# Retention output product with seven products on half of its rows, the residual stream kept off chip during the mixer

## The chip, the cores and the metric

The kernel runs on one core of a Trainium2 chip. The metric is the device time of one execution in microseconds (us). Three executions of the kernel before took 1260.34 to 1261.17 us, median 1260.89 us. The engines are TensorE (PE; PEld is its weight load), VectorE (DVE), ScalarE (ACT), GpSimd (POOL) and SyncE (SP, which issues most DMAs).

## What is computed

Two decoder layers over 256 tokens of width 1024, in float32. Each layer normalises the residual stream `h`, runs a retention mixer and a state-space mixer side by side, merges them by gates, adds the result to `h`, and then does a gated feed-forward block:

```python
def hybrid_mixer(h, w_in, ret_out, ..., ssd_out, w_o):
    u = h @ w_in
    q, k, v, g_ret, z, xbc, dt, gate_ret, gate_ssd = jnp.split(u, ...)
    ...
    o_ret = yr @ ret_out
    ...
    o_ssd = ys @ ssd_out
    merged = jax.nn.sigmoid(gate_ret) * o_ret + jax.nn.sigmoid(gate_ssd) * o_ssd
    return merged @ w_o

def reference(x, ...):
    h = x
    for l in range(DEPTH):
        h = h + hybrid_mixer(rmsnorm(h, norm_mix_w[l]), ...)
        h = h + swiglu(rmsnorm(h, norm_ffn_w[l]), w_gate_up[l], w_down[l])
    return rmsnorm(h, final_norm_w)
```

The change concerns `o_ret = yr @ ret_out`: 256 tokens x 2048 times 2048 x 1024.

## The kernel before

**Exact products from three.** Every float32 operand is split into a high part (rounded to float32r, on ACT) and the rest (on DVE), and a product is the sum of three matmuls, high-high, high-low and low-high (`mm3`, L538). A matmul has a 128x128 stationary tile of the activations and 512 columns of a weight. Weights are read from HBM in pieces of 128x1024 (512 KB) into `raw` tiles and split on the way: `wh` by ACT (L502), `wl` by DVE (L523). Six split pieces are held at once (`hlS`), and four raw ones (`rawS`).

**Seven products for eight.** Some of the products already use Strassen's scheme in Winograd's form on a 2x2 block partition: the 256 tokens as two halves, eight row tiles of the weight as two quarters of four, 1024 columns as two halves. Seven block products named 11, t1, t2, 22, t3, 21, t4 take the place of eight, and sums of weight quarters and of operand blocks are made beforehand: `sevens` (L355) lays out the pieces, `wino_sums` (L402) makes the weight sums (t1 and t2 by DVE; those listed in `added` by a DMA of the POOL queue that adds into the tile, L412), `seven_sums` (L671) makes the operand sums on DVE and ACT, `seven` (L840) issues the products. `out_wino` (L1031) is the form for a product with sixteen (or more) row tiles, of which eight go by seven products and the others are plain: the state-space output product (`SMID`, L296) and the down projection (`AMID`, L294) use it. A `*` in these lists is one plain row tile, between the products.

**The retention output product** uses `out_job` (L986, called at L1676): 16 row tiles x 2 token halves x 2 column halves x 3 = 192 matmuls of 512 columns. `ret_post` (L1668) multiplies each result by the gate `sgr`. It comes after the four `g` jobs, which make its operand `yr`, and before the four `z` jobs; the state-space products, `ssd` and `wo`, follow.

**Order of the work.** The order is worked out when the program is built: `Flow` (L72) plays each step as a generator with a modelled cost and a priority, and each engine takes the ready step of the lowest priority number. The result is one fixed in-order list per engine; on the chip the engines only wait for each other's semaphores. Jobs are listed in `MIXER` (L1124). Chunk work of the state-space scan (`ssd_chunk`, L1575) has the low priority `lp = pr + 8` (L1564), so it fills what is left. The feeder (L474) issues weight loads on the SP queue in one fixed order, each when its slot is free.

**Memory.** PSUM has six `acc` banks (`accS`) and two `tr` banks (`trS`, for transposes). `h` (L272) stays on chip all the time, two tiles of 128x1024; the decay tables of the retention lie in `cst` (L273) all the time. Operand sums for the mixer's seven products use slots named "C". `ssd_post` (L1743) ends the merge: multiply, add, and transpose (`transposed`, L627) into the operand of `wo`; `add_to` (L1789) adds to `h` and starts the norm of the next block (`Norm.half`, L727).

Of the kernel before, what the change touches and what calls it, by code (L numbers as in the profile page):

```python
# [9 lines left out]
F32 = mybir.dt.float32  # L10
# [6 lines left out]
P = 128  # L17
# [175 lines left out]
def trunk_kernel(  # L193
# [3 lines left out]
    ssd_out, w_o, norm_ffn_w, w_gate_up, w_gf, w_sw, w_dw, w_down, final_norm_w, consts, out,  # L197
# [4 lines left out]
    SLOW = 1500.0  # L202
    ZS_PR = 1.0
    PR0, SLACK = 1.6, 2500.0
    BESIDE = (8, 10, 12, 14, 11, 11, 9, 24, 44)
# [66 lines left out]
    h = [cp.tile([P, D], F32, tag=f"h{t}", name=f"h{t}") for t in range(NT)]  # L272
    cst = cp.tile([P, K_N], F32, tag="cst", name="cst")  # L273
# [22 lines left out]
    SMID = ("*", "*", "11", "*", "t1", "*", "t2", "22", "*", "t3", "21", "t4")  # L296

# [57 lines left out]
    def sevens(w1, w2, added=("t3",), order=ALONE, slots=None):  # L355
# [4 lines left out]
        def add(of):  # L360
# [8 lines left out]
            for q, need, sl in (("11", ("11",), (segS, new_raw_seg)), ("12", ("t1", "t3"), (zS, new_z)),  # L369
                                ("22", ("t2", "22"), (rawS, new_raw)), ("21", ("21",), (rawS, new_raw))):  # L370
                need = [c for c in need if c not in added or c not in ("t1", "t2")]
                for i in range(2):
                    land = holder(held[q, i])
                    if (q, i) == ("11", 1):
                        land = then(land, [wino_sums(i, of, evs, turn, held, part, added, zS) for i in range(2)])
# [26 lines left out]
    def wino_sums(i, job, evs, turn, held, part, added, zS):  # L402
# [51 lines left out]
        fl.release(segS)  # L454
# [254 lines left out]
    class Norm:  # L709


        def __init__(self, w, tag=None):
            self.tag = tag
            self.plain = [[Event() if tag else None for _ in range(NT)] for _ in range(2)]
# [12 lines left out]
        def half(self, t, n, pr):  # L727

            nsl = slice(n * 512, (n + 1) * 512)
            fl.spawn(self.square(t, n, pr))  # L730
            wb = yield self.wb[n]
# [8 lines left out]
            fl.release(silS)  # L740

# [395 lines left out]
    def add_layer_jobs(l):  # L1137
# [15 lines left out]
        for m in MIXERS[l]:  # L1153
            if m == ("ssd",):
# [42 lines left out]
    early_par = Event()  # L1197

    def layer(l, mix, nxt, opening=None):
# [81 lines left out]
        def steps():  # L1281
# [5 lines left out]
            ax, sr, pol, dtt, la = small("ax"), small("sr"), small("pol"), small("dtt"), small("la")  # L1287
# [15 lines left out]
            yield stt(n, pr, dtt, dps, 0.0, pol, ALU.max, ALU.add)  # L1303
            yield stt(n, pr, v3(la), v3(dtt), -1.0, ea.unsqueeze(1).broadcast_to([P, NT, NH]), ALU.mult, ALU.mult)
# [407 lines left out]
        def z_job(g):  # L1712
# [3 lines left out]
            if g == 2:  # L1716
                fl.spawn(seven_sums(zops, yz, (0, 1), "A", at_job[0] + ZS_PR))
# [375 lines left out]
```

## Time and profile before

| | |
|---|---|
| median of three runs | 1260.89 us |
| the profiled execution's own time | 1260.23 us |
| its span in the profile | 1258.2 us |
| granted TensorE clock, mean | 0.999 of full |
| instructions | 17517 |
| moved by DMA | 258.13 MB, 205 GB/s on average |
| POOL busy | 64.4 us |

The span is what the trace covers, from the first to the last instruction; the execution's own time has 2.0 us more around it. Matmuls overlap in the trace (one lasts 0.39 us, the next starts 0.23 us after it), so a PE that is busy all the time can still have gaps between starts: for PE the distance from start to start is read, not the busy time alone.

### The profile page before, as it was taken

The page shows a single profiled execution, that of the slowest core. Times are in us where ns is not written, and L with a number is a line of the kernel's source. Part 1 is how long each engine was busy: PE and PEld are TensorE (multiplying, and loading weights), DVE is VectorE, ACT ScalarE, POOL GpSimd, SP SyncE. Part 2 cuts the span into 40 slices and gives each one's busy share as a digit, 9 for nine tenths or more (in the row PEclk, how much of TensorE's full clock was granted, in tenths as well). Part 3 has the DMA queues.
Part 4 walks back from the last instruction along what each step waited for, and adds up shares of the span by engine and source line. Part 5 has one row for each costly group of instructions (what it writes and reads, how often), then busy time and mean ns, then how long its engine had stood idle before and what let it go on. Part 6 is the DMA issues. An engine that isn't in the chain of part 4 may idle for free.

```text
span 1258.2 us, 17517 instructions
## 1 busy us (share of the span) xinstructions
PE 1247.1 (99%) x6306; PEld 1055.3 (84%) x6306; DVE 1062.3 (84%) x1452; ACT 851.0 (68%) x1271; POOL 64.4 (5%) x84
## 2 busy tenths in 40 slices
PE   9999999999999999999999999999999999999997
PEld 7889888888888788888888898888888887888886
DVE  6998978878589978999788888878875998888996
ACT  6876786987376566776586676967954664766754
POOL 0000000000012001011000000000000110010010
PEclk9999999999999999999999999999999999999999
DMA  8668555555475757886766485555555765678873
GB/s 292 222 176 292 178 175 160 175 189 196 154 281 148 230 177 225 296 225 207 229 210 226 123 266 166 172 192 167 187 199 170 242 189 201 206 226 254 271 202 113
DMA packets 73606, 258.13 MB, mean 205 GB/s; under 512 B 8464, under 2 KB 8720, under 8 KB 73520
## 3 DMA queue, kind: packets, MB, share of 16 engines
q1 hardware_dynamic: 66832, 233.32, 54.6%
q0 software_dynamic: 6400, 23.18, 9.8%
q8 instruction: 49, 0.80, 0.2%
q10 hardware_dynamic: 288, 0.52, 0.1%
q14 instruction: 37, 0.30, 0.1%
HBM read 255.88 MB, written 1.11 MB: 204 GB/s over the span
## 4 chain that ended last, share of the span: by engine, by line
PE 86%; DVE 8%; DMA 3%; issue 2%; ACT 1%; SPq 0%; POOL 0%; POOLq 0%; ACTq 0%; DVEq 0%
PE acc L540 17%; PE acc L539 17%; PE acc L541 17%; PE acc L962 16%; PE acc L963 9%; DVE wl L523 4%; PE tr L636 2%; PE acc L965 2%; PE yps L1623 2%; DVE raws L229 1%; DMA raws<-in_w_sw_dram 1%; DMA raw<-in_w_dw_dram 1%; DMA raw<-in_ssd_out_dram 1%; DVE D L229 1%; DVE plain L229 1%
## 5 line engine op out<-in xcount | busy, mean ns | idle before, releaser
L523 DVE TENSOR_TENSOR wl<-raw,wh 128x1024 fp32r<-128x1024 f32 (+2 forms) x392 | 464.5, 1194 | 76.1 <-ACT wh L502 73.7
L502 ACT ACTIVATE wh<-raw 128x1024 fp32r<-128x1024 f32 (+2 forms) x392 | 400.9, 1036 | 186.2 <-PE acc L541 87.3
L962 PE MATMUL acc<-xT,wh 128*128 128x512 f32 x840 | 304.1, 400 | 0.0
L963 PE MATMUL acc<-xT,wl 128*128 128x256 f32 x960 | 252.2, 281 | 0.0
L539 PE MATMUL acc<-wh,xT 128*128 128x512 f32 (+1 forms) x568 | 219.5, 386 | 0.0
L541 PE MATMUL acc<-wh,xT 128*128 128x512 f32 (+1 forms) x568 | 216.0, 380 | 0.0
L540 PE MATMUL acc<-wl,xT 128*128 128x512 f32 (+1 forms) x568 | 216.0, 380 | 0.0
L963 PEld LDWEIGHTS acc<-xT,wl 128*128 128x128 f32 x960 | 181.2, 189 | 10.1
L962 PEld LDWEIGHTS acc<-xT,wh 128*128 128x128 f32 x840 | 158.0, 188 | 32.3
L540 PEld LDWEIGHTS acc<-wl,xT 128*128 128x128 f32 x568 | 106.7, 188 | 20.1 <-issue 1.0
L539 PEld LDWEIGHTS acc<-wh,xT 128*128 128x128 f32 x568 | 106.7, 188 | 19.5 <-issue 1.2
L541 PEld LDWEIGHTS acc<-wh,xT 128*128 128x128 f32 x568 | 106.7, 188 | 19.5
L502 ACT ACTIVATE wh<-raws 128x1024 fp32r<-128x1024 f32 x80 | 84.1, 1057 | 45.1 <-DVE raws L229 23.6
L523 DVE TENSOR_TENSOR wl<-raws,wh 128x1024 fp32r<-128x1024 f32 x80 | 96.3, 1218 | 9.2 <-ACT wh L502 9.1
L539 PE MATMUL acc<-wh,A 128*128 128x512 f32 x224 | 89.0, 397 | 0.0
L541 PE MATMUL acc<-wh,A 128*128 128x512 f32 x224 | 87.3, 390 | 0.0
L540 PE MATMUL acc<-wl,A 128*128 128x512 f32 x224 | 87.2, 389 | 0.0
L232 DVE SCALAR_TENSOR_TENSOR cc<-cc,cv 128x255 f32<-128x255 f32 (+1 forms) x144 | 68.3, 477 | 11.5 <-ACT cc L222 10.4
L539 PE MATMUL acc<-wh,C 128*128 128x512 f32 (+1 forms) x184 | 72.2, 392 | 0.0
L540 PE MATMUL acc<-wl,C 128*128 128x512 f32 (+1 forms) x184 | 71.2, 387 | 0.5 <-DVE wl L523 0.3
L541 PE MATMUL acc<-wh,C 128*128 128x512 f32 (+1 forms) x184 | 70.7, 384 | 0.0
L541 PEld LDWEIGHTS acc<-wh,A 128*128 128x128 f32 x224 | 42.1, 188 | 9.0
(183 smaller groups left out, 1889.0 us busy)
## 6 DMA issues: line engine op xcount, KB each, us to landing
raw<-in_w_tm_dram SPq DMA_DIRECT2D x104, 512.0 KB, 4.2
raw<-in_w_fm_dram SPq DMA_DIRECT2D x80, 512.0 KB, 4.0
raw<-in_w_gf_dram SPq DMA_DIRECT2D x40, 512.0 KB, 4.7
raw<-in_ret_out_dram SPq DMA_DIRECT2D x32, 512.0 KB, 3.8
raw<-in_w_gate_up_dram SPq DMA_DIRECT2D x32, 512.0 KB, 6.0
raw<-in_w_down_dram SPq DMA_DIRECT2D x28, 512.0 KB, 4.4
raw<-in_w_gr_dram SPq DMA_DIRECT2D x24, 352.0 KB, 3.8
seg<-acs SPq DMA_DIRECT2D x16, 512.0 KB, 5.1
```

The lines of the kernel that those rows point to most:

```text
L229: return dve(n, pr, lambda: nc.vector.tensor_tensor(out=out, in0=in0, in1=in1, op=op))
L232: return Op("dve", 1.04 * n + 130, lambda: nc.vector.scalar_tensor_tensor(out=out, in0=in0, scalar=scalar, in1=in1, op0=op0, op1=op1), pr)
L502: nc.scalar.activation(out=wh[:, :m], in_=raw[:, :m], func=AF.Copy)
L523: nc.vector.tensor_tensor(out=wl[:, :m], in0=raw[:, :m], in1=wh[:, :m].bitcast(F32), op=ALU.subtract)
L539: nc.tensor.matmul(ps, lhsT=lh, rhs=rh, start=first, stop=False, **kw)
L540: nc.tensor.matmul(ps, lhsT=lh, rhs=rl, start=False, stop=False, **kw)
L541: nc.tensor.matmul(ps, lhsT=ll, rhs=rh, start=False, stop=last, **kw)
L636: nc.tensor.transpose(out=ps[:, j * P : (j + 1) * P], in_=src[:, j * P : (j + 1) * P], identity=ident)
L962: nc.tensor.matmul(a, lhsT=wh[:, k % 4, fsl], rhs=x[:, k % 4, :, :], start=k == 0, stop=False)
L963: nc.tensor.matmul(a[:, :SEQ], lhsT=wl[:, k % 4, fsl], rhs=xh[:, k % 4, :], start=False, stop=False)
L965: nc.tensor.matmul(a, lhsT=wh[:, k % 4, fsl], rhs=x[:, k % 4, :, :], start=False, stop=True)
L1623: nc.tensor.matmul(ps[:, i * HD : (i + 1) * HD], lhsT=sg[:, i, :], rhs=xdt[:, i * HD : (i + 1) * HD], start=True, stop=True)
```

## The change

The retention output product goes through `out_wino`: row tiles 0 to 7 by seven products, 8 to 15 plain, in the order `RMID`; 11's raw quarters get two slots of their own (`dec`), which hold the decay tables earlier in the layer. Its operand sums use four new slots "O". `h` lies in two of the "O" slots and gives them up once the norm before the mixer has read it: layer 0 reads it again from `x`, layer 1 writes it to HBM first and reads it back, both on the SP queue, at the start of the `ssd` job. The norm's own operand sums move from "C" to "O". The decay tables are loaded per layer. `ret_post` adds the gated sums that `add_r` left in `gated`. Chunk products of groups 2 and 3 use `tr` banks. The transposes of `ssd_post` are put 800 ns later in the modelled order (`MT_SLACK`). [...]

```diff
-    BESIDE = (8, 10, 12, 14, 11, 11, 9, 24, 44)
+    SLOW, MT_SLACK = 1500.0, 800.0
+    ZS_PR, SAVE, DEC_AT = 1.0, 2000.0, 9000.0
+    BESIDE = (8, 10, 12, 14, 11, 11, 9, 24, 44, 46)
+    decS, new_dec = pooled(tp, (P, D), F32, "dec", 2)
-    bigS = {k: Sem(4) for k in ("A", "C", "D", "Y")}
+    bigS = {k: Sem(4) for k in ("A", "C", "D", "O", "Y")}
-    h = [cp.tile([P, D], F32, tag=f"h{t}", name=f"h{t}") for t in range(NT)]
-    cst = cp.tile([P, K_N], F32, tag="cst", name="cst")
+    h = [None] * NT
+    cst = cp.tile([P, K_DEC], F32, tag="cst", name="cst")
+    RMID = ('*', '*', '*', '*', '11', '*', 't1', '*', 't2', '22', '*', 't3', '21', 't4')
+    RET_FIRST, RET_APART, RET_PR = (decS, new_dec), (), 0.0
...
     class Norm:
+            self.kept = drp.tile([NT, P, D], F32, tag="kept", name="kept", bufs=1) if saved else None
+            self.reads = 8 if saved else 4
...
+        def read(self):
+            self.reads -= 1
+            if not self.reads and self.tag == "O":
+                for t in range(NT):
+                    fl.release(bigS["O"])
+
+        def save(self, t, nsl, pr):
+            yield SAVE
+            yield Op("sp", 450, lambda: nc.sync.dma_start(out=self.kept[t][:, nsl], in_=h[t][:, nsl]), pr)
+            yield fl.transfer(4 * P * 512, 2048)
+            self.read()
...
+            if m == ("ret",):
+                group(sevens(w_rw[l, 0], w_rw[l, 1], added=("t3", "t4"), order=RMID, first=RET_FIRST),
+                      plain((out_srcs(ret_out[l])[8:], RET_APART)))
...
+        def load_decays():
+            if l:
+                yield DEC_AT
+            yield decS
...
-                yield accS
+                yield (trS if g >= 2 else accS)
...
+        def g_job(hd):
+            if hd == 2:
+                fl.spawn(seven_sums(rops, yr, (0, 1), "O", at_job[0] + RET_PR))
+            return tm_job(xT, g_post(hd))
...
         def ret_post(t, n, ps, j):
+            nsl = slice(n * 512, (n + 1) * 512)
+            yield tt(512, j, sgr[t][:, nsl], ps, sgr[t][:, nsl], ALU.mult)
+            fl.release(accS)
+            yield tt(512, j, sgr[t][:, nsl], sgr[t][:, nsl], gated[t].value[:, nsl], ALU.add)
...
+        def add_r(t, n, u, j):
...
+            yield tt(512, j, to[:, nsl], u, sgr[t][:, nsl], ALU.mult)
-        run["ret"] = lambda: out_job(yr, 16, ret_post)
+        run["ret"] = lambda: out_wino(yr, 16, 0, "O", RMID, ret_post, add_r, rops)
...
-            yield from transposed(sgr[t][:, nsl], 4, mT, n, t, j - 1)
+            yield from transposed(sgr[t][:, nsl], 4, mT, n, t, j - 1, slack=MT_SLACK)
...
+        def restore(t):
+            pr = at_job[0]
+            yield bigS["O"]
+            def emit():
+                h[t] = new_big("O", F32, (P, D))
+                nc.sync.dma_start(out=h[t], in_=mix.kept[t] if mix.saved else x[0, t * P : (t + 1) * P, :])
+            yield Op("sp", 450, emit, pr)
...
         def ssd_job():
+            for t in range(NT):
+                fl.spawn(restore(t))
...
             def post(t, n, ps, j):
+                yield h_ev[t]
                 yield tt(512, j - 1, h[t][:, nsl], h[t][:, nsl], ps, ALU.add)
...
-        norms = [Norm(norm_mix_w[0], "C"), Norm(norm_mix_w[1], "C"), Final(final_norm_w)]
+        norms = [Norm(norm_mix_w[0], "O"), Norm(norm_mix_w[1], "O", saved=True), Final(final_norm_w)]
...
+    out["w_rw"] = cols(a["ret_out"][:, :1024], [0, 512], 512, 2)
...
-    nc = _bacc.Bacc("TRN2", target_bir_lowering=False, num_devices=1)
+    nc = _bacc.Bacc("TRN2", target_bir_lowering=False, num_devices=1, dynamic_dma_scratch_size=8192)
```

## Rows read from the trace of the kernel before

**Rows 1.** The page's part 1: busy time, share of the span, instructions.

```profile
PE 1247.1 (99%) x6306; PEld 1055.3 (84%) x6306; DVE 1062.3 (84%) x1452; ACT 851.0 (68%) x1271; POOL 64.4 (5%) x84
```

**Rows 2.** Timeline of PE, layer 0, end of the retention output product; x16 is chunk work.

```profile
320.55 1.89 PE L1623 MATMUL yps<-xdt,seg 128*128 128x64 f32 x16
...
323.03 0.40 PE L539 MATMUL acc<-wh,A 128*128 128x512 f32 x1
...
338.02 0.39 PE L539 MATMUL acc<-wh,xT 128*128 128x512 f32 x1
```

**Rows 3.** Groups of DVE and of ACT by form: busy us, mean ns, idle before.

```profile
L523 DVE TENSOR_TENSOR wl<-raw,wh 128x1024 fp32r<-128x1024 f32 x364 | 441.2, 1220 | 71.3 <-ACT wh L502 68.9
...
L229 DVE TENSOR_TENSOR plain<-plain 128x512 f32<-128x512 f32 x32 | 21.9, 684 | 2.0 <-ACT plain L222 2.0
...
L229 DVE TENSOR_TENSOR raws<-raws,cc 128x1024 f32<-128x1024 f32 x16 | 19.5, 1216 | 0.0
...
L502 ACT ACTIVATE wh<-raw 128x1024 fp32r<-128x1024 f32 x364 | 380.6, 1057 | 175.9 <-PE acc L541 82.8 <-DMA raw<-in_w_tm_dram 16.3 <-PE acc L962 13.3
...
L222 ACT ACTIVATE sx<-acc 128x512 f32<-128x512 f32 x30 | 17.7, 590 | 4.8 <-PE acc L541 4.7
```

**Rows 4.** Busy time by stretch: PE, PEld, DVE, ACT, POOL, clock, DMA share, GB/s.

```profile
260.00:280.00 20.00, 20.00 (x115) 17.38 (x115) 13.92 (x23) 16.27 (x35) 0.00 (x0) 1.00 0.46 155
280.00:325.00 45.00, 45.00 (x234) 37.74 (x233) 35.55 (x43) 28.89 (x44) 0.00 (x0) 1.00 0.61 200
325.00:345.00 20.00, 20.00 (x90) 16.57 (x89) 10.26 (x11) 6.70 (x7) 0.00 (x0) 1.00 0.40 127
345.00:380.00 35.00, 35.00 (x164) 29.09 (x164) 29.97 (x42) 24.58 (x37) 4.90 (x7) 1.00 0.77 276
380.00:424.00 44.00, 43.40 (x200) 35.75 (x198) 42.91 (x52) 28.66 (x37) 6.71 (x7) 1.00 0.65 180
...
901.00:946.00 45.00, 45.00 (x235) 37.72 (x234) 35.21 (x43) 27.82 (x43) 0.00 (x0) 1.00 0.59 194
946.00:966.00 20.00, 20.00 (x90) 16.56 (x89) 10.09 (x11) 7.03 (x7) 0.00 (x0) 1.00 0.39 135
```

**Rows 5.** Timeline of PE at the merge of either layer, brackets: idle before.

```profile
423.01 0.39 PE L541 MATMUL acc<-wh,C 128*128 128x512 f32 x1
424.46 0.63 PE L636 MATMUL tr<-cst,D 128*128 128x128 f32 x4 [1.06 <-DVE D L229]
...
1044.65 0.39 PE L541 MATMUL acc<-wh,C 128*128 128x512 f32 x1
1045.96 0.63 PE L636 MATMUL tr<-cst,D 128*128 128x128 f32 x4 [0.92 <-DVE D L229]
```

**Rows 6.** The chain of waits ahead of those transposes: start, us, what.

```profile
396.43 2.27 DVE raws L229 x2
...
408.41 7.54 DMA raw<-in_ssd_out_dram
...
1024.35 9.59 DMA raws<-in_w_sw_dram
```

**Rows 7.** Timeline of PE inside the state-space product's seven products, layer 1.

```profile
1036.19 0.39 PE L541 MATMUL acc<-wh,Y 128*128 128x512 f32 x1
1036.59 0.50 PE L539 MATMUL acc<-wh,Y 128*128 128x512 f32 x1
```

**Rows 8.** DMA issues by line: how many, size, median us to landing.

```profile
cc<-in_w_sw_dram POOLq DMA_DIRECT2D x4, 512.0 KB, 5.5
raws<-in_w_sw_dram POOLq DMA_DIRECT2D x4, 512.0 KB, 8.2
```

**Rows 9.** Timeline of POOL in the state-space output product, layer 0.

```profile
390.27 0.90 POOL L412 DMA_DIRECT2D cc<-in_w_sw_dram  x1
...
400.98 0.86 POOL L412 DMA_DIRECT2D raws<-in_w_sw_dram  x1 [8.88 <-DVE wl L523]
403.00 0.86 POOL L412 DMA_DIRECT2D raws<-in_w_sw_dram  x1 [1.17 <-DVE wl L523]
```

More of the change, by code (lines that the diff above doesn't have):

```diff
@@ L196, in trunk_kernel @@
     x, x_t, norm_mix_w, w_tm, w_gr, w_fm, conv_p, steps_p, ret_out, ssd_norm_w,
[L197 removed]
+    ssd_out, w_o, norm_ffn_w, w_gate_up, w_gf, w_rw, w_sw, w_dw, w_down, final_norm_w, consts, out,
 ):
@@ L353, in add_job, with sevens @@
         group(plain((srcs, apart)))
-    def sevens(w1, w2, added=("t3",), order=ALONE, slots=None):
+    def sevens(w1, w2, added=("t3",), order=ALONE, slots=None, first=None):
         def add(of):
@@ L368, in add @@
             got_specs = []
-            for q, need, sl in (("11", ("11",), (segS, new_raw_seg)), ("12", ("t1", "t3"), (zS, new_z)),
+            for q, need, sl in (("11", ("11",), first or (segS, new_raw_seg)), ("12", ("t1", "t3"), (zS, new_z)),
                                 ("22", ("t2", "22"), (rawS, new_raw)), ("21", ("21",), (rawS, new_raw))):
@@ L374, in add @@
                     if (q, i) == ("11", 1):
-                        land = then(land, [wino_sums(i, of, evs, turn, held, part, added, zS) for i in range(2)])
+                        land = then(land, [wino_sums(i, of, evs, turn, held, part, added, zS, (first or (segS,))[0]) for i in range(2)])
                     got_specs.append((min(at[c, i] for c in need) - (0.01 if q == "12" else 0),
@@ L400, in then, with wino_sums @@
         return run
-    def wino_sums(i, job, evs, turn, held, part, added, zS):
+    def wino_sums(i, job, evs, turn, held, part, added, zS, xS):
         pr = job - 0.7
@@ L1398, in retention @@
             fl.release(accS)
+            heads_left[0] -= 1
+            if not heads_left[0]:
+                fl.release(decS)
             yield act(3 * P, pr, ph, prb, AF.Copy)
@@ L1436, in layer @@
         heads = [(Event(), Event(), Event()) for _ in range(RH)]
+        heads_left, decays = [RH], Event()
+        def load_decays():
[3 more added lines that the diff above has]
+            def emit():
+                d = new_dec()
+                nc.sync.dma_start(out=d, in_=consts[:, K_DEC:])
+                return d
+            d = yield Op("sp", 450, emit, -1)
+            fl.transfer(4 * P * D)
+            fl.set(decays, d)
+        if l:
+            fl.spawn(load_decays())
+        else:
+            first_decays.append(load_decays)
         def q_job(hd):
@@ L1768, in layer, with emit @@
         zops = {q: Event() for q in ALONE}
+        h_ev = [Event() for _ in range(NT)]
+        def restore(t):
+            pr = at_job[0]
+            yield bigS["O"]
+            def emit():
+                h[t] = new_big("O", F32, (P, D))
+                nc.sync.dma_start(out=h[t], in_=mix.kept[t] if mix.saved else x[0, t * P : (t + 1) * P, :])
+            yield Op("sp", 450, emit, pr)
+            yield fl.transfer(4 * P * D)
+            fl.set(h_ev[t])
         def ssd_job():
@@ L1784, in seven_job @@
         def seven_job(kind, c, added):
+            if kind == "z":
+                z_begins(c)
             return wino_job(mix.ops, posts_of[kind](c), posts_of[kind](c + 1))
@@ L1990, in whole @@
         yield from opening.slots()
+        for t in range(NT):
+            yield bigS["O"]
+            h[t] = new_big("O", F32, (P, D))
         def constants(lo, hi):
```

54 lines of the change are left out of this document (34 added, 20 removed).

## The prediction

> **What bounds the kernel now.** The page's first part comes first: PE is busy for 1247.1 of 1258.2 us, DVE for 84%, ACT for 68% [rows 1]. A busy PE may still have gaps, so the second view is PE's timeline. From 323.03 to 338.02 us there are 66 steps from start to start: 0.227 us for a matmul of 512 columns, and nothing between them [rows 2]. PE is the bound, at its own pace: a matmul less is 0.227 us less, as long as whatever feeds PE keeps up. [...]
>
> **The sum, step by step.** *Matmuls.* Before: 16 row tiles x 4 x 3 = 192 per layer. After: 8 x 4 x 3 = 96 plain and 7 products x 4 row tiles x 3 = 84, together 180. Over two layers 24 fall away: 24 x 0.227 = **-5.45 us**, all on the path. [...]
>
> *Work on DVE and ACT, per layer.* DVE: 22 pieces are split instead of 16, 6 x 1.22 = 7.3 us; t1 and t2 of two pieces each, 4 x 1.22 = 4.9; operand sums, 12 steps x 0.68 = 8.2 (four to join the parts, four sums, four low parts); two subtractions, four gatings in add_r and four more additions in ret_post, 10 x 0.68 = 6.8: 27.2 us in all [rows 3]. ACT: 6 x 1.06 + 7 x 0.59 = 10.5 us [rows 3], against 29.4 us idle from 280 to 345 [rows 4]: nothing. For DVE the cover is its idle time from 260 to 380 us, 30.3 us, less the 2.7 us by which the stage shrinks: 27.6 [rows 4]. So 27.2 fit into 27.6, if the chunk work of groups 2 and 3 gives way into the stretches behind; it has the lowest priority and is wanted only by z2 and z3, behind z0 and z1. That is the narrow point of the change. What PE loses by it lies between nothing and the whole of what cannot move (first rival). The nearest row is another stage of the same kind under a fuller DVE: within the seven products of the state-space output, PE's longest step is 0.40 instead of 0.227 us [rows 7]. I take about two such, 0.4 us per layer: **+0.8 us**.
>
> *Merge.* There PE's gaps are 1.45 and 1.31 us from start to start [rows 5], so 2.3 us above its pace are lost. MT_SLACK moves the transposes 0.8 us back in the modelled order, so a step of three matmuls (0.68 us) goes ahead of them, perhaps two. One each: **-1.4 us**, between 0 and -2.3. What is late next is wo, whose operand these transposes make; plain work of the state-space product still stands before it. In return DVE enters 380 us with less slack behind it: the chain into these transposes runs over DVE sums and over DMAs that took 7.54 and 9.59 us [rows 6], and every microsecond of DVE work left over from the retention product ends there. Between 0 and some 2 us per layer; I take 0.5: **+1.0 us**.
>
> *Transfers.* Plain bytes of ret_out stay equal (8 pieces and 8 quarter pieces for 16). New per layer are two loads of h (1.05 MB) at the start of ssd, in layer 1 also four saves of h and one load of the decay tables. At 276 GB/s for a share of 0.77 [rows 4], the two loads of h take 2.9 us of all DMA engines; the stretch from 380 to 424 has 35% of its DMA time free [rows 4]. So 0, with 2.9 us per layer as the other end. On SP they stand in front of the pieces that ssd and wo still want. Their slots have been free since the end of the retention product, so SP does not stand still for them; the saves wait for DVE's last addition to h, behind which layer 1's weights queue, but they are ordered 2 us after it, and six split and four raw pieces cover a hitch there. h is wanted only when wo ends. On POOL's queue come four adding DMAs per layer; POOL is otherwise idle from 260 to 345 us [rows 4]. They land 5.5 and 8.2 us after issue [rows 8]; t3 and t4 stand last in the order and have that time. [...] Issue took 0.86 us both for the first and the second of a pair 2.0 us apart [rows 9], so nothing waits now; the other end is a second one that starts only when the first has landed, 6.2 us later. I take 0, the value of those rows.
>
> *Banks.* Chunk products in the `tr` banks hold one for 1.9 us [rows 2] and a DVE step of 0.68: transposes behind it could lose up to 2.6 us per layer, and the freed `acc` banks are what the seven products need. Nothing either way. The last plain row tile is 12 matmuls, 2.7 us, in which add_r must free a bank for z0: one or two DVE steps, so nothing.
>
> Sum: -5.45 + 0.8 - 1.4 + 1.0 = **-5.05 us**. The profiled execution took 1260.23 us in all (span 1258.2 and 2.0 around it); it becomes 1255.2. The median of the runs lies 0.66 us above that execution, so the forecast is **1255.8 us**.
>
> **Rivals.** *DVE becomes the bound in the retention product (slower).* Operand sums, splits and weight sums, 20.4 us, are due before the last product starts. In 280 to 325 us only 9.5 are idle [rows 4]; the 6.1 us before it are scattered while the operands are still being made. If the chunk work does not give way, for instance because its buffers (four `sx`, also used by the operand sums and by the products' copies) are held in the wrong order, PE waits up to 10.9 us per layer: -5.45 + 21.8, 1277.2 us. At half of it, 5.5 us per layer, -5.45 + 11.0, the time is 1266.4. It decides from 4.0 us of waiting per layer on. For it: the fit of 27.2 into 27.6. Against it: DVE is idle for 9.7 us directly behind the stage in both layers, and the state-space stage runs with 1.1 us idle of 44 and loses next to nothing within its products [rows 4, 7].
>
> *The gain is given back at the merge (no change).* The left-over work, 2 us per layer, runs through z and ssd, where DVE has no room, and the later transposes don't help: -5.45 + 0.8 + 4.0, so 1260.2. For it: the chain there is DVE's from 396 us on [rows 6]. Against it: 5.0 us are idle from 345 to 380 [rows 4].
>
> *The adding DMAs come late (no change).* POOL's issues of 0.86 to 0.90 us were made while DVE was busy for 42.9 of 44 us [rows 4, 9], so they weren't held up visibly. If each of the eight were held by one DVE step of 1.22 us, and a pair's second by the first's, half of 9.8 us would show on PE: -5.05 + 4.9, 1260.7. [...]
>
> *h or the weights come late, or the change takes out less than it counts (no change).* 2.9 us per layer: -5.05 + 5.8, 1261.6. That fewer than 24 matmuls go is hardly possible, as the lists are fixed when the program is built.
>
> **How the numbers follow.** About 0.2%, 2.5 us, can be told from no change. Forecast 0.66 (1253 to 1258.3; its low end takes all of the merge's 2.3 us and no new loss: -7.75, 1253.1); gain given back at the merge 0.16; adding DMAs late 0.03; transfers late or nothing taken out 0.03; DVE the bound 0.12. Faster therefore 0.66, within 0.2% 0.22, slower 0.12. The range from 1253.0 to 1263.0 leaves out the first rival and little of the forecast's own low end. The forecast's own range is 1253.0 to 1258.3.
>
> **What would show it.** Right: PE's instructions fall by 24, from 6306 to 6282; PE's steps in the retention product stay at 0.227 us with single steps up to 0.4; DVE's busy time grows by about 54 us, and from 260 to 424 us it is idle for 2 or 3 us; the gap before the merge's first transposes falls below 1 us. Wrong: waits of PE for `wl` pieces or for operand sums in the retention product (first rival), a gap of more than 3 us at the merge (second), ACT or DVE waiting for the adding DMA's tile ahead of t3 or t4 (third), SP standing at the saves or loads of h.

## The result, and the profile after

The changed kernel takes 1263.13 us (median of 22 runs, 1260.83 to 1265.72); the kernel before 1260.20 us (22 runs). The ratio is 1.0021, 95% interval 1.0015 to 1.0027: **slower by 0.2%**, where 5 us less were forecast. The profiled execution took 1262.38 us, its span is 1260.5 us (before: 1258.2). What follows is read from that execution; it lies 0.75 us below the median of the 22.

First the page's part 1 of the changed kernel, beside [rows 1]:

```profile
PE 1244.5 (99%) x6282; PEld 1049.6 (83%) x6282; DVE 1106.7 (88%) x1516; ACT 873.7 (69%) x1299; POOL 73.9 (6%) x92
```

The 24 matmuls are gone (6306 to 6282), and DVE has 44.4 us more. So the saving was made, and something took more than it back. Where it went is read from PE's timeline, by two stages in each layer: **stage A** from the first matmul of the retention output product to the first of the state-space product (the retention product and the four z jobs), **stage B** from there to the first matmul of `wo` (the state-space product and the merge). The marks of stage A in layer 0, of the kernel before:

```profile
284.09 0.39 PE L539 MATMUL acc<-wh,Y 128*128 128x512 f32 x1
...
384.26 0.39 PE L539 MATMUL acc<-wh,C 128*128 128x512 f32 x1
```

and of the changed kernel:

```profile
283.81 0.39 PE L544 MATMUL acc<-wh,A 128*128 128x512 f32 x1
...
385.95 0.39 PE L544 MATMUL acc<-wh,C 128*128 128x512 f32 x1
```

Stage A took 384.26 - 284.09 = 100.17 us before and takes 102.14 after, though it has 12 matmuls less, 2.72 us at 0.227. The same marks in layer 1 give 100.22 and 102.81. **So 4.7 and 5.3 us are lost in stage A, 10.0 us together.** Stage B became shorter, 43.89 to 42.58 us and 44.02 to 42.68, 2.65 us together. -5.45 + 10.0 - 2.65 = +1.9 us; the span grew by 2.3, so 0.4 us lie outside the two stages.

What PE waits for stands in its waits (engine, line, released by: us in total, times, longest, over the whole execution); the changed kernel:

```profile
PE acc L544 <- ACT sx L222: 4.5, 2, 2.9
PE acc L545 <- DVE wl L528: 1.5, 4, 0.7
...
PE ips L1662 <- DVE xdt L229: 1.0, 2, 0.9
```

The first is new and the largest: once per layer PE stands until ACT has copied a bank (`sx`), in the middle of the product t4. PE's timeline at the two places (brackets: idle before, and who ended it):

```profile
326.07 0.39 PE L546 MATMUL acc<-wh,Y 128*128 128x512 f32 x1
328.08 0.50 PE L544 MATMUL acc<-wh,Y 128*128 128x512 f32 x1 [1.62 <-ACT sx L222]
...
948.27 0.39 PE L546 MATMUL acc<-wh,Y 128*128 128x512 f32 x1
951.58 0.50 PE L544 MATMUL acc<-wh,Y 128*128 128x512 f32 x1 [2.92 <-ACT sx L222]
```

From start to start these are 2.01 and 3.31 us, 4.9 us above PE's pace: half of the loss. Of the other half, PE's remaining waits in stage A (one for a `wl` in z0, at 340.29, two for the scan's `xdt`, two for an operand from ACT) take 2.4 us, four more transposes per layer 0.6, and some 2 us are single steps longer by hundredths and tenths of a microsecond, with no wait recorded ahead of them. The copy is not slow (0.58 us); it is late. ACT's timeline in layer 0 shows what stands ahead of it in ACT's list:

```profile
304.80 1.06 ACT L507 ACTIVATE wh<-raw 128x1024 fp32r<-128x1024 f32 x1 [1.21 <-DMA raw<-in_w_rw_dram]
...
312.82 1.06 ACT L507 ACTIVATE wh<-raw 128x1024 fp32r<-128x1024 f32 x1 [4.20 <-DMA raw<-in_ret_out_dram]
...
319.76 1.06 ACT L507 ACTIVATE wh<-raw 128x1024 fp32r<-128x1024 f32 x1 [1.16 <-DMA raw<-in_w_rw_dram]
322.21 1.06 ACT L507 ACTIVATE wh<-raw 128x1024 fp32r<-128x1024 f32 x1 [1.39 <-PE acc L545]
323.18 1.99 ACT L507 ACTIVATE wh<-dec 128x1024 fp32r<-128x1024 f32 x2
325.19 1.28 ACT L222 ACT_TABLE_LOAD   x1
326.48 1.06 ACT L222 ACTIVATE seg<-seg 128x1024 f32<-128x1024 f32 x1
327.44 0.58 ACT L222 ACTIVATE sx<-acc 128x512 f32<-128x512 f32 x1
```

Three times ACT stands for a weight piece that has not landed (1.21, 4.20 and 1.16 us; in layer 1 the second of these is 5.71). When it goes on, it has splits, a table load and the scan's exponential to do before the copy, since its list is fixed. The pieces are late because their loads are issued late; SP's timeline:

```profile
285.33 0.33 SPq L489 DMA_DIRECT2D raw<-in_ret_out_dram  x1
294.44 6.07 SPq L489 DMA_DIRECT2D raw<-in_w_rw_dram  x2
308.86 0.33 SPq L489 DMA_DIRECT2D raw<-in_ret_out_dram  x1
...
311.13 4.36 SPq L489 DMA_DIRECT2D raw<-in_w_rw_dram  x2
```

The piece that ACT waits for until 312.82 was asked for at 308.86. The row at 294.44 is two loads; the second, the last before 308.86, went out at 300.18. A load goes out when a raw slot is free, and a slot is free when DVE has made `wl` of the piece in it. DVE's timeline:

```profile
290.93 1.22 DVE L528 TENSOR_TENSOR wl<-dec,wh 128x1024 fp32r<-128x1024 f32 x1
292.06 1.22 DVE L229 TENSOR_TENSOR dec<-dec,raw 128x1024 f32<-128x1024 f32 x1
293.20 1.22 DVE L528 TENSOR_TENSOR wl<-raw,wh 128x1024 fp32r<-128x1024 f32 x1
294.33 1.22 DVE L229 TENSOR_TENSOR dec<-dec,raw 128x1024 f32<-128x1024 f32 x1
...
298.93 1.22 DVE L528 TENSOR_TENSOR wl<-raw,wh 128x1024 fp32r<-128x1024 f32 x1
...
307.61 1.22 DVE L528 TENSOR_TENSOR wl<-raw,wh 128x1024 fp32r<-128x1024 f32 x1
```

Each of the three loads follows the end of such a `wl` at once (293.20, 298.93 and 307.61, each plus 1.22). One round of a slot can be read from these lines: load issued at 300.18, ACT's split begun at 304.80 and done at 305.86, `wl` begun at 307.61 and done at 308.83, next load at 308.86. Of these 8.7 us the load took 4.6, the split 1.1, `wl` itself 1.2, and 1.75 us are DVE's delay, as it had other steps to do first. And there are few slots: the two quarters "12" stay in two of the four raw slots until t1 and t3 have been made from them, so all other retention pieces go through the two that are left. **The reading**: two rotating slots, with a round of 8.7 us of which a DVE that is behind makes 1.75; late loads; ACT's list held up; the copy, and PE, late. Part of the lateness is in the transfers: the load at 311.13, beside an adding DMA that POOL issued at 310.26, was in flight for 8.6 us, until ACT could split it at 319.76, and in the kernel before no load of this product took more than 5.3 us. No run separates that part.

DVE's and ACT's room is in the view by stretch, in the columns of [rows 4]; the changed kernel:

```profile
260.00:280.00 20.00, 20.00 (x115) 17.39 (x115) 16.79 (x24) 16.05 (x33) 0.00 (x0) 1.00 0.64 224
280.00:325.00 45.00, 44.88 (x219) 36.79 (x218) 40.95 (x53) 33.36 (x47) 4.05 (x5) 1.00 0.69 196
325.00:345.00 20.00, 17.73 (x77) 13.82 (x76) 19.62 (x24) 14.22 (x21) 0.00 (x0) 1.00 0.58 190
345.00:380.00 35.00, 34.84 (x176) 28.86 (x175) 33.41 (x48) 23.80 (x37) 5.93 (x7) 1.00 0.83 278
380.00:424.00 44.00, 44.00 (x203) 36.56 (x203) 43.38 (x54) 29.01 (x38) 6.68 (x7) 1.00 0.72 209
```

In the 164 us DVE is busy for 154.2 and idle for 9.9. It was never "full" as a sum; it is full where it counts, 19.62 of 20 us behind t4, and late before. At the merge the waits of [rows 5] are gone: the first transposes follow a matmul after 0.24 us in layer 0, and after 0.30 in layer 1.

```profile
425.41 0.39 PE L546 MATMUL acc<-wh,C 128*128 128x512 f32 x1
425.65 0.63 PE L641 MATMUL tr<-cst,D 128*128 128x128 f32 x4
```

### The profile page after: what moved, and what is told of

It is laid out like the page before. It is cut to its first block, busy times and chain, and to the rows that moved or that the text cites. A ratio compares the mean times of both kernels' runs of the same rounds, so it can differ in the third digit from the quotient of the medians.

```text
span 1260.5 us, 17612 instructions
## 1 busy us (share of the span) xinstructions
PE 1244.5 (99%) x6282; PEld 1049.6 (83%) x6282; DVE 1106.7 (88%) x1516; ACT 873.7 (69%) x1299; POOL 73.9 (6%) x92
## 4 chain that ended last, share of the span: by engine, by line
PE 80%; DVE 8%; ACT 4%; DMA 4%; issue 3%; SPq 0%; POOLq 0%; POOL 0%; ACTq 0%; DVEq 0%
PE acc L545 16%; PE acc L544 16%; PE acc L546 16%; PE acc L986 14%; PE acc L987 8%; DVE wl L528 4%; DMA raw<-in_w_tm_dram 2%; PE tr L641 2%; PE acc L989 2%; PE yps L1675 2%; ACT wh L507 2%; DVE D L229 1%; DVE raws L229 1%; DMA raw<-in_w_dw_dram 1%; PE ips L1662 1%
## 5 line engine op out<-in xcount | busy, mean ns | idle before, releaser
L507 ACT ACTIVATE wh<-raw 128x1024 fp32r<-128x1024 f32 (+2 forms) x388 | 396.8, 1035 | 154.2 <-PE acc L546 27.3
L507 ACT ACTIVATE wh<-raws 128x1024 fp32r<-128x1024 f32 x80 | 84.2, 1057 | 41.1 <-DVE raws L229 22.2
L544 PE MATMUL acc<-wh,C 128*128 128x512 f32 (+1 forms) x152 | 59.3, 390 | 0.2 <-ACT wh L507 0.2
L545 PE MATMUL acc<-wl,C 128*128 128x512 f32 (+1 forms) x152 | 58.4, 384 | 0.3 <-DVE wl L528 0.2
L546 PE MATMUL acc<-wh,C 128*128 128x512 f32 (+1 forms) x152 | 58.2, 383 | 0.0
```

The costliest lines, as they stand in the source:

```text
L507: nc.scalar.activation(out=wh[:, :m], in_=raw[:, :m], func=AF.Copy)
L544: nc.tensor.matmul(ps, lhsT=lh, rhs=rh, start=first, stop=False, **kw)
L545: nc.tensor.matmul(ps, lhsT=lh, rhs=rl, start=False, stop=False, **kw)
L546: nc.tensor.matmul(ps, lhsT=ll, rhs=rh, start=False, stop=last, **kw)
```

## The experiments

Fifteen kernels, each timed beside the kernel before on the same chip (11 runs each, but 4 of e3, 5 of e7, e13 and e15, and 7 of e4 and e8). "Loss in A" is the time of stage A in both layers above 194.92 us, which is twice 100.18 (the plain product) less twice 2.72. All figures are of the profiled executions, but for the ratio. One execution of a kernel differs from another by 1 us and more: the profiled one lies 3.4 us above the median of its kernel's runs in e4, 2.2 in e7, 1.2 in e8, 1.1 in e15 and 0.8 in e11, and 0.8 us below it in e6. So the loss in A of e4 and of e7 is that of a long execution.

| kernel | A, layer 0 and 1 | loss in A | B, layer 0 and 1 | span | ratio to before, interval |
|---|---|---|---|---|---|
| changed | 102.14, 102.81 | 10.0 | 42.58, 42.68 | 1260.5 | 1.0021 [1.0015, 1.0027] |
| e1, plain | 100.17, 100.22 | | 42.79, 42.74 | 1256.7 | 0.9994 [0.9985, 1.0003] |
| e2, plain | 100.18, 100.45 | | 42.88, 42.52 | 1256.4 | 0.9994 [0.9985, 1.0003] |
| e3 | 111.08, 109.91 | 26.1 | 43.62, 43.76 | 1277.3 | 1.0164 [1.0150, 1.0178] |
| e4 | 102.88, 104.15 | 12.1 | 43.52, 42.67 | 1263.3 | 1.0025 [1.0013, 1.0036] |
| e5 | 100.22, 99.96 | 5.3 | 44.85, 43.40 | 1256.9 | 0.9990 [0.9981, 0.9998] |
| e6 | 100.06, 101.11 | 6.3 | 42.56, 42.59 | 1255.8 | 0.9989 [0.9980, 0.9998] |
| e7 | 104.30, 104.66 | 14.0 | 42.51, 42.71 | 1264.1 | 1.0035 [1.0022, 1.0048] |
| e8 | 101.89, 100.30 | 7.3 | 44.69, 45.63 | 1263.2 | 1.0029 [1.0017, 1.0040] |
| e9 | 102.11, 102.58 | 9.8 | 42.57, 42.86 | 1259.4 | 1.0014 [1.0005, 1.0023] |
| e10, plain | 100.18, 100.48 | | 42.52, 42.58 | 1254.9 | 0.9980 [0.9971, 0.9989] |
| e11 | 99.40, 98.46 | 2.9 | 44.67, 43.91 | 1256.1 | 0.9977 [0.9969, 0.9986] |
| e12 | 99.94, 99.28 | 4.3 | 44.15, 44.91 | 1257.1 | 0.9993 [0.9984, 1.0002] |
| e13 | 98.60, 98.03 | 1.7 | 44.82, 42.70 | 1253.0 | 0.9961 [0.9949, 0.9974] |
| e14, plain | 100.18, 100.23 | | 42.54, 42.54 | 1255.0 | 0.9978 [0.9969, 0.9987] |
| e15 | 99.27, 99.69 | 4.0 | 42.57, 42.57 | 1254.3 | 0.9965 [0.9953, 0.9978] |

A limit: e5, e8, e10 and e12 change what the planner sees, so the whole order of the work is another, beside the one size changed. No run has a fifth slot in the changed kernel's own order. In e4 and e7 the order of the product itself is edited. e6, e9 and e15 keep every engine's list of the changed kernel, e11 and e13 that of e5, and e14 that of e10, but for the widths of DVE's steps.

### What the other parts of the change do

**e1: the kernel before with the later transposes alone.**

```diff
-            yield from transposed(sgr[t][:, nsl], 4, mT, n, t, j - 1)
+            yield from transposed(sgr[t][:, nsl], 4, mT, n, t, j - 1, slack=800.0)
```

> The kernel before with the 0.8 us on the merge's transposes alone. The merge's gain is separate from the rest: PE's gaps before the first transposes (1.45 and 1.31 us in the kernel before) fall below 0.5 us and the time falls by 2 to 2.7 us, a ratio near 0.998. Rival: the step only moves the wait to the product behind it (wo), and the time stays within 0.5 us of the kernel before.

Stage B falls by 1.1 and 1.28 us, 2.4 together, and the span by 1.5: the step does about what the changed kernel shows at the merge. The time fell less than expected: the ratio was to be near 0.998, and at 0.9994 it can't be told from no change.

**e2: the changed kernel with the plain retention product.**

```diff
-        run["ret"] = lambda: out_wino(yr, 16, 0, "O", RMID, ret_post, add_r, rops)
+        run["ret"] = lambda: out_job(yr, 16, ret_post)
```

> The changed kernel with the retention output product as 16 plain row tiles again; the residual stream off chip, the tables per layer, the tr banks and the later transposes stay. Theory that the loss is all in the new product and its surroundings: as fast as the kernel before with the later transposes alone, ratio 0.998 (within 0.6 us of it). Rival, the residual stream's transfers or the tr banks cost: 1 to 5 us more than that, ratio 0.999 to 1.002.

Stage A is that of the kernel before (100.18 and 100.45), and the span is e1's within 0.3. So the residual stream off chip, the tables per layer and the chunk products in the `tr` banks cost nothing that shows, and **the loss belongs to the seven products**.

### Attempts on the wait for the copy

**e3: the held quarters "12" in `cc` slots, so that all four raw slots rotate.**

```diff
-                group(sevens(..., order=RMID, first=RET_FIRST),
+                group(sevens(..., order=RMID, first=RET_FIRST, slots=(ccS, new_cc)),
```

> The changed kernel with the retention's held quarters (12) loaded into the two cc slots instead of two of the four raw slots. Theory 'late pieces' (held quarters leave two raw slots, ACT waits for weights, 4.2 and 5.7 us, and reaches the copy that t4 needs too late): those waits of ACT fall below 1.5 us, the gaps before t4 (2.0 and 3.3 us) fall below 0.6, and 4 to 6 us come back: 1257 to 1259 us, ratio 0.9975 to 0.999. Theory 'DVE is full': no change, 1263, ratio 1.002. Theory 'scan work ahead of the copy': the gaps before t4 stay above 1.5 us, ratio 1.001 to 1.002.

Far worse. SP's timeline says why: the `cc` slots are held by the convolutions then, and SP, which issues in a fixed order, stands at that load with all later pieces behind it.

```profile
276.69 26.35 SPq L489 DMA_DIRECT2D cc<-in_w_rw_dram  x2
```

This answers nothing about the slots; it shows what a late piece costs when it stands first in the queue.

**e4: a plain row tile between 21 and t4 instead of ahead of 11**, so that PE has 2.7 us of other work while ACT comes to the copy.

```diff
-    RMID = ('*', '*', '*', '*', '11', '*', 't1', '*', 't2', '22', '*', 't3', '21', 't4')
+    RMID = ('*', '*', '*', '11', '*', 't1', '*', 't2', '22', '*', 't3', '21', '*', 't4')
```

> The changed kernel with one plain row tile moved from the front to between 21 and t4, so that the copy has 2.7 us more. Both 'late pieces' and 'scan work ahead of the copy': the gaps before t4 (2.0 and 3.3 us) go, 3 to 5 us come back (1258 to 1260, ratio 0.9985 to 1.0), while ACT's waits for weights stay. 'DVE is full': the wait only moves, to t4's weights or to z0: 1262 to 1264, ratio 1.0015 to 1.003.

The wait for the copy goes, and PE waits for weights instead:

```profile
PE acc L545 <- DVE wl L528: 4.3, 7, 1.0
```

Five of the seven waits, 3.4 us, stand in stage A, and two of 0.63 us for ACT's split beside them. The wait was the place where lateness came out, not its source. How much the move is worth this trace doesn't tell: its execution took 1265.38 us, the longest of seven (median 1261.99), and has a stretch at a lower granted clock in it, 0.72 (last section).

**e7: the sum for t1 too by an adding DMA, which takes two of DVE's sums per layer away.**

```diff
-                group(sevens(..., added=("t3", "t4"), order=RMID, first=RET_FIRST),
+                group(sevens(..., added=("t1", "t3", "t4"), order=RMID, first=RET_FIRST),
```

> The changed kernel with t1 of the retention product also made by an adding DMA, so that the held quarters (12) are loaded only for t3 and occupy no raw slot before; DVE has 2 additions (2.3 us) less per layer. 'Late pieces': ACT's waits for the plain pieces and the gaps before t4 fall below 1 us, 4 to 6 us come back: 1257 to 1259 us, ratio 0.9975 to 0.999. 'DVE is full': 1 to 2 us come back, ratio 1.0005 to 1.0015. If the longer row of DMAs (load 12, add 22) is late, the gap stands before t1 or t3 instead and the time stays at 1262 or more.

Slower: the weights of t3 and z0 come late then (5.6 us in four waits for `wl`), and ACT waits 8.0 and 8.9 us for quarter pieces. DVE's work was swapped for DMA latency.

**e8: the scan's last group started with z0 instead of with the retention product.**

```diff
-            if jj == 1:
+            if jj == 1 and g < 3:
...
+                fl.spawn(ssd_group(3))
```

> The changed kernel with the scan work of group 3 started with z0 instead of after its xs job, out of the retention product. 'Scan work ahead of the copy': the gaps before t4 fall below 0.6 us; the waits in z (0.2 to 0.9 us before the scan's products) grow by 1 to 3 us; 1260 to 1263 us. 'Late pieces': ACT still waits 4 us and more for the plain pieces; the gaps shrink by the 2.3 us of table load and exponential at most; 1261 to 1264 us. 'DVE is full': about 10 us of DVE work leave the stage, so its waits go and come back in z2 and z3, 1262 to 1268 us.

The waits for the copy fall to 0.63 us in each layer, but the same scan work comes back as waits in z and the state-space product: stage B is 2.1 and 2.95 us longer than in the changed kernel. So the scan's exponential ahead of the copy is not enough of a cause by itself.

### Slots and DVE

**e5: five raw slots**, and with them half the room for the descriptors of POOL's DMAs, 4096 bytes instead of 8192.

```diff
-    HB, RB, TAIL, WARM = 6, 4, 5, 2
+    HB, RB, TAIL, WARM = 6, 5, 5, 2
...
-    nc = _bacc.Bacc("TRN2", target_bir_lowering=False, num_devices=1, dynamic_dma_scratch_size=8192)
+    nc = _bacc.Bacc("TRN2", target_bir_lowering=False, num_devices=1, dynamic_dma_scratch_size=4096)
```

> The changed kernel with five raw slots instead of four (its 4 KB from the descriptor room, 4096 bytes). 'Late pieces' (two of four raw slots hold quarters, so loads wait for splits): SP issues the plain pieces of the retention product earlier, ACT's waits for them (4.2 and 5.7 us) and the gaps before t4 fall below 1 us, 3 to 6 us come back: 1257 to 1260 us, ratio 0.9975 to 1.0. 'DVE is full': 1262 to 1264 us, ratio 1.0015 to 1.003. If the smaller descriptor room costs anything, POOL's issues take more than 0.93 us or adding DMAs land later than 8 us, and everything gets slower.

The wait for the copy is gone, and so are ACT's for the plain retention pieces; the loss in A falls from 10.0 to 5.3 us, by the slot together with the order that goes with it. What PE waits for now is DVE's scan operands in stage A, and weights in stage B:

```profile
PE ips L1662 <- DVE xdt L229: 2.7, 3, 1.4
PE acc L545 <- DVE wl L528: 1.4, 2, 0.8
```

**e9: the smaller descriptor room alone** (the last line of that diff).

> The changed kernel with the descriptor room of POOL's DMAs at 4096 bytes instead of 8192, and nothing else: every engine's list is the same. The run with a fifth raw slot had this smaller room too. If its gain of 4.5 us against the changed kernel is the slot's (with the new order that goes with it), this kernel stays with the changed one: span 1260.5 us within 1, the two waits of PE for ACT's copy ahead of t4 still there (1.6 and 2.9 us in the changed kernel). If the smaller room had a part in it, the waits are shorter and the span is below 1259 us.

The two waits for the copy stay (1.42 and 2.31 us), and so does the loss in A, 9.8 us; the span, 1259.4, lies 0.1 us outside the expected band. The room has no part in e5's gain.

**e10: five slots with the plain product** (e2 and e5 together), the control.

> Control: a fifth raw slot and the smaller descriptor room, with the retention product left as plain (16 row tiles), beside the residual stream off chip, the tables and the later transposes. If the slot mends what the seven products brought into the retention product, it gives nothing here, where nothing waits: span 1256.4 us within 0.8, as in the run with the plain product and four slots. If the slot helps any kernel of this kind, the span falls by 2 us or more, and the gain of the run with the fifth slot says nothing of the new product.

Neither answer whole: the span falls by 1.5 us, but stage A doesn't move (100.18 and 100.48). The gain is at the start of the program: the retention product of layer 0 begins at 282.56 us instead of 283.89 (282.19 to 283.28 in the six kernels with five slots, 283.38 to 284.64 in the others). So of e5's 3.6 us of span some 1.5 are that, and within stage A the slot helps the seven products alone, by 4.7 us. This is also the fastest kernel here that computes all of the reference.

**e6: lighter sums on DVE, four slots.** DVE's sums for t1 and t2 and its four operand sums are made on 8 columns, by the author's estimate 7 us of DVE less per layer.

```diff
-                yield tt(D, pr, x, x, w, ALU.add)
+                yield dve(D, pr, lambda n=8 if xS is decS else D: nc.vector.tensor_tensor(out=x[:, :n], in0=x[:, :n], in1=w[:, :n], op=ALU.add))
...
-            yield tt(512, pr, out, a, b, op_)
+            yield dve(512, pr, lambda ..., n=512 if tag != "O" or plain else 8: ...)
```

> The changed kernel with every engine's order kept and DVE's work shortened: the additions for t1 and t2 and the four operand sums of the retention product touch 8 columns instead of 1024 and 512, 4 x 1.15 + 4 x 0.6 = 7 us of DVE less per layer (those sums are left out of the result). 'DVE is full': the gaps before t4 (2.0 and 3.3 us) and in z go, 4 to 8 us come back: 1255 to 1259 us, ratio 0.9955 to 0.999. 'Late pieces' by slots and transfers alone: less than 1.5 us comes back, 1261.5 to 1263, ratio above 1.0005. Both together (loads wait for slots that DVE frees late): 2 to 5 us.

The copy's wait goes in layer 0 and halves in layer 1, and the loss in A falls to 6.3 us, though ACT still stands for the two retention pieces:

```profile
ACT wh L507 <- DMA raw<-in_ret_out_dram: 11.3, 2, 5.8
```

So in layer 0 the late piece alone no longer makes PE wait for the copy; in layer 1 it still does, for 1.4 us. With every list kept, this is what DVE's load alone is worth: 3.8 us. It does free the slot earlier, the load of the late piece in layer 0 goes out at 305.87 instead of 308.86; but that load is in flight longer, and ACT starts on it at 311.74 instead of 312.82.

**e11: both cures** (e5 and e6 together).

> Both cures together: the fifth raw slot, and DVE's sums for t1 and t2 and its four operand sums of the retention product on 8 columns instead of 1024 or 512 (that part of the product's sums is left out of the result; DVE's list is that of the run with the fifth slot). If the whole loss is the supply of weights and operands by a full DVE, the two cures take away the waits that are left (PE for DVE's xdt and wl, 4 us in the run with the fifth slot), and the span is 1252 to 1254 us. If one cure only does what the other does, 1255.5 to 1257 us. If something else than the supply holds PE (the retention products themselves at a longer step), also 1255.5 or more, with no waits of PE above 0.5 us left from 280 to 385 us.

The cures add for the most part: the loss in A is 2.9 us (5.3 and 6.3 with one of them), so 7.1 us come back, where 4.7 and 3.8 would make 8.5. But the span is 1256.1 us, in the band of "one does what the other does": stage B became 44.67 and 43.91, where the backlog now comes out. By the span of this one execution the run would have been misread; the ratio, 0.9977 against 0.9990 and 0.9989, shows some of the second cure.

**e12: five slots and the scan's last group later** (e5 and e8 together), an attempt at a better version.

> A version that may beat both: the fifth raw slot, and the chunk work of the scan's last group started with z0 instead of with the retention product. With five slots the longest wait left in layer 0 is PE's for DVE's xdt of the chunk work, 1.39 us inside the retention product. If the chunk work is in the way there, that wait goes and the span falls from 1256.9 to about 1255 us. If the same DVE work only comes later, as it did with four slots, the waits stand in the z and state-space products instead: 1256.5 to 1259 us.

As e5: less loss in A, the waits in stage B instead.

**e13 and e14: much room on DVE, with seven products and with the plain product.** To e11 and to e10 is added that the scan's and z's steps that work in place take 8 columns.

```diff
-            yield tt(1024, lp, sg, sg, cb[:, 2 * t, :].unsqueeze(1).broadcast_to([P, HPG, P]), ALU.mult)
+            yield tt8(1024, lp, sg[:, 0, :], sg[:, 0, :], cb[:, 2 * t, :], ALU.mult)
...
-                yield tt(512, j, sil, sil, y, ALU.mult)
+                yield tt8(512, j, sil, sil, y, ALU.mult)
```

> Five raw slots and a DVE with room: as the run with both cures, and besides in each layer the scan's steps that work in place (its 1024-wide multiplication, and of the 512-wide ones four per group) and z's two multiplications per result on 8 columns, some 30 us of DVE less per layer; every other engine's list is the same, and those parts of the scan, of z and of the retention sums are left out of the result. P is the span of its pair, the plain product with the same room on DVE. If the loss is the supply by a full DVE, wherever it shows, the 24 matmuls now bring what they are worth: P - 4.5 to P - 5.5 us (24 x 0.227 = 5.45). If the seven products cost PE something else (longer steps by themselves, ACT's list, weights from HBM, the start of the product), the span is P - 2 or more, as it was P + 1.2 with both cures.

> The pair of the run before: the plain retention product with five raw slots, and the same steps of the scan and of z on 8 columns (left out of the result); every other engine's list as in the control with the plain product. PE waited for next to nothing in that control, so room on DVE should give nothing by either theory: span 1254.9 us within 0.8. If the span falls by 2 us or more, DVE costs the plain product's kernel something too, and the pair is to be read by its difference alone.

The view by stretch over stage A, first of e13, then of e14:

```profile
284.00:333.00 49.00, 48.88 (x229) 40.13 (x229) 43.11 (x60) 39.13 (x52) 4.05 (x5) 1.00 0.73 215
333.00:385.00 52.00, 52.00 (x266) 43.74 (x265) 36.14 (x67) 35.08 (x58) 4.59 (x8) 1.00 0.55 201
```

```profile
284.00:333.00 49.00, 49.00 (x252) 41.05 (x251) 25.24 (x39) 24.61 (x38) 0.00 (x0) 1.00 0.53 172
333.00:385.00 52.00, 52.00 (x243) 43.24 (x242) 37.83 (x58) 34.98 (x51) 6.11 (x8) 1.00 0.74 253
```

The plain product gains nothing from the room (1255.0, as expected). With seven products stage A is 1.58 and 2.20 us shorter than its pair's, 3.8 of 5.45 us, and the loss there is 1.7. The span is 2.0 us below its pair's, where the second answer begins: by it the 24 matmuls don't yet bring what they are worth. The difference is in stage B of layer 0, 2.3 us longer than the pair's: there PE waits twice for a `wl`,

```profile
398.39 0.39 PE L544 MATMUL acc<-wh,A 128*128 128x512 f32 x1
399.42 0.50 PE L545 MATMUL acc<-wl,A 128*128 128x512 f32 x1 [0.64 <-DVE wl L528]
```

as it does in e5 and e11, whose order this is. It is not in stage B of e15, with another order and the same room, so it goes with the planner's order for five slots; why there was not tried.

**e15: the same room with four slots, in the changed kernel's own order** (e6 with the edits of e13).

> The changed kernel with its own four raw slots, with DVE's room of the two runs before and the light sums; every other engine's list is that of the changed kernel. If slots are scarce only because DVE frees them late, this kernel does about as well as the one with five: within 1.5 us of it, and ACT's waits for the late retention pieces (5.5 and 5.8 us with the light sums alone) and PE's for the copy ahead of t4 are gone. If two rotating slots are too few by themselves, ACT still waits over 3 us for those pieces and the span stays at 1254 us or more.

Mixed. The span is within 1.3 us of e13's, and the medians, 1254.93 and 1254.76 us, don't differ by more than the runs of one kernel do. PE's wait for the copy is gone in layer 0 and is 1.37 us in layer 1. ACT still stands for the retention piece in both, 4.70 and 5.44 us. The profile puts the first down to PE, but the piece itself landed at 311.82, 0.1 us before ACT went on. ACT's timeline:

```profile
311.93 1.06 ACT L507 ACTIVATE wh<-raw 128x1024 fp32r<-128x1024 f32 x1 [4.70 <-PE acc L545]
...
930.72 1.06 ACT L507 ACTIVATE wh<-raw 128x1024 fp32r<-128x1024 f32 x1 [5.44 <-DMA raw<-in_ret_out_dram]
```

So room on DVE takes back 6.0 of the 10.0 us of stage A without the slot; with it, 8.3, by one execution of each. With two rotating slots the piece stays late with all the room that DVE was given here: they are a limit of their own.

## Why the prediction was wrong

**Where it held.** The bound was PE's step of 0.227 us, and 24 matmuls went. The changed kernel's steps without a wait are 0.227 us as before (twelve of them from 1045.62 us on take 2.72). The transfers of `h`, the saves and tables, POOL's issues and the banks were taken at nothing, and e2 and e9 show nothing (spans of 1256.4 us against 1256.7 in e1, and of 1259.4 against 1260.5 in the changed kernel). Nor is a delay of the adding DMAs' issues under a fuller DVE seen: POOL's two adding DMAs into `dec` in the retention product of layer 0 were issued in 0.86 us each while DVE was busy for 40.95 of 45 us:

```profile
305.65 0.86 POOL L417 DMA_DIRECT2D dec<-in_w_rw_dram  x1 [8.70 <-DVE wl L528]
310.26 0.86 POOL L417 DMA_DIRECT2D dec<-in_w_rw_dram  x1 [3.75 <-DVE wl L528]
```

**Where a size was off for the better.** The merge was taken at -1.4 + 1.0 = -0.4 us and gave -2.65: the later transposes took nearly all of the 2.3 us, and the backlog that was to come out there did not (it does in the five-slot runs).

**The step that failed** is *Work on DVE and ACT*: "27.2 fit into 27.6", from which +0.8 us followed. It was 10.0 us, and it came by a path that the prediction doesn't have: loads that wait for two rotating slots, ACT standing 4.20 and 5.71 us at a piece in flight, and PE standing 4.9 us above its pace for ACT's copy, with 5.1 us more in the rest of stage A. Three statements fell:

1. *Idle time was taken as cover.* The sum was even too high: DVE grew by 44.4 us, 22.2 per layer, not 27.2, and kept 9.9 us idle where 2 to 3 were foretold. PE still lost 5.0 us per layer, because a late `wl` is more than a late operand: it also frees the slot for the next load, so its lateness (1.75 us of the round shown above) goes round through SP, DMA and ACT. e13 and e14 show the other side: with room on DVE 8.3 of the 10.0 us come back (slot included), and the plain product doesn't care.
2. *ACT: "nothing".* ACT had 17.4 us idle from 280 to 345 us after the change, yet PE's largest wait was on it: 4.20 of the 17.4 were spent standing at one piece in flight (5.71 in layer 1), with all else of its list behind it.
3. *"six split and four raw pieces cover a hitch there"* (under *Transfers*). Said of the saves, and not asked of the retention product, where two of the four raw slots are held. e5 gives 4.7 us in stage A for a fifth slot with the order that goes with it.

The nearest row that was chosen for the price, a step of 0.40 us in the state-space product [rows 7], came from a product whose held quarters lie in slots of their own. That was the difference to look for.

**The rival that came nearest** is the first, DVE as the bound in the retention product: 5.0 us per layer, above the 4.0 from which it was to decide; it was given 0.12. The argument against it was idle time behind the stage, once more a sum. But its mechanism came true only in part. Its sign, PE waiting for `wl` or for operand sums in the retention product, hardly shows there: PE stood for ACT's copy, and its one recorded wait for a `wl` in stage A, 0.65 us, is in z0. DVE's load by itself is worth 3.8 us (e6) to 6.0 (e15) of the 10.0, and postponing the scan alone (e8) did not cure it. The second rival, the loss at the merge, did not happen. Nor did the third as it was told: no engine waits for an adding DMA into `dec`; whether these DMAs lengthen the loads in flight beside them is not shown. Of the fourth, weights did come late, but not behind the loads of `h`.

**What stays open**: 1.7 us in stage A of e13 (0.7 of them are the four more transposes per layer; no wait of PE above 0.1 us is left there, though ACT still waits 5.1 us for quarter pieces); what the fifth slot gives without its new order; what the longer flights cost; and stage B of layer 0 in the five-slot order. The median of the changed kernel grew by 0.6 us more than the span. Its 22 executions have a mean granted clock of 0.995 to 0.999, where those of the kernel before beside the experiments have 0.998 or 0.999; the profiled one has 0.999, so whether the clock took part in that isn't shown.

## What to carry to other kernels

A second bound is not judged by its idle time in the stage but by what its lateness holds up: ask which engine frees the slot that the next load waits for, how many of the slots rotate while others are held, and what stands in the in-order list behind the piece that will be late. When a wait goes and the time stays, cut the timeline into stages at marks that both kernels have: here the gain of a cure in one stage came out in part as a loss in the next (e8, e11), and the span alone hid both.

## What the runs showed of the hardware that was not expected

In e4 and e7 PE ran slower for a while after a stand. In e4, in layer 1, seven steps from 952.22 to 955.21 us are 0.43 us instead of 0.227, behind two waits of 0.63 and 0.96 us, and the granted clock by stretch (the last column but two) is below 1.00 there, 0.89 and 0.72.

```profile
948.00:953.00 5.00, 3.41 (x11) 2.24 (x11) 4.45 (x6) 5.00 (x7) 0.00 (x0) 0.89 0.65 211
953.00:957.00 4.00, 4.00 (x14) 3.17 (x13) 4.00 (x5) 4.00 (x11) 0.00 (x0) 0.72 0.44 155
957.00:962.00 5.00, 5.00 (x24) 4.14 (x23) 4.67 (x7) 3.90 (x6) 0.00 (x0) 1.00 0.76 270
```

At 0.2 us each they add 1.4 us to the waits themselves. Of e4's seven executions the three with a mean granted clock of 0.997 or 0.998 took 1264.55 to 1265.38 us (this one is among them), and the four with 0.999 took 1261.35 to 1261.99. e7 has such a run in z0 behind a wait of 2.01 us, with a granted clock of 0.57 from 341 to 345 us. But in the changed kernel PE stood for 2.92 us, was busy for no more than 2.66 of the 5 us from 946 on, and kept the clock, 1.00:

```profile
946.00:951.00 5.00, 2.66 (x12) 1.88 (x10) 4.83 (x5) 4.97 (x6) 0.00 (x0) 1.00 0.84 270
951.00:954.00 3.00, 2.42 (x11) 2.00 (x12) 3.00 (x4) 3.00 (x5) 0.00 (x0) 1.00 0.30 67
```

So the length of a stand alone does not tell here whether the clock falls; what does was not tried.

In the lines of the changed kernel above, DVE's steps cost less back to back than their own duration: 1.22 us each, but 1.13 to 1.14 from start to start (292.06, 293.20, 294.33). For the 32 steps that came per layer, 0.08 us each, that would be 2.6 of the 5.0 us by which the sum of durations was too high, an estimate from these three lines; where the rest went is not shown.
